# Rounded three-pass matmuls for seven tiles of a state-space input projection, with the places of its input and of its tables' scratch exchanged

## The chip, the cores and the metric

The kernel runs on one core of one Trainium2 chip. A core has a matrix engine (TensorE, PE in the profile; its weight loads are listed as PEld), VectorE (DVE), ScalarE (ACT), GpSimd (POOL) and SyncE (SP), which here only issues transfers. Each engine works through its own queue of instructions in order and waits for others by semaphores. The on-chip memory is SBUF; matmuls write into PSUM, and the other engines read their results from there. The metric is the device time of one execution in microseconds; the median of several runs counts.

## The reference, cut to what matters

Two residual layers, the first with a state-space mixer, the second with attention, each followed by a gated convolutional network. The model width is 1024 and the sequence 512 long, all in float32. The part that the change touches is the very first sub-layer:

```python
def modulate(x, g, shift, scale):
    return rmsnorm(x, g) * (1.0 + scale) + shift

def s5_mixer(h, w_in, lam_re, lam_im, log_dt, b_re, b_im, c_re, c_im, d_skip, w_glu, w_out):
    u = h @ w_in
    ug = u.reshape(Bsz, S, S5_GROUPS, S5_GROUP)
    dt = jnp.exp(log_dt.astype(f32))[:, None]
    mag = jnp.exp(lre * dt)
    lb_re = mag * jnp.cos(lim * dt)
    lb_im = mag * jnp.sin(lim * dt)
    ...
    _, ys = lax.scan(chunk_step, h0, u_chunks)
    y = y + d_skip.astype(f32) * u.astype(f32)
    y = jax.nn.gelu(y)
    y = y * jax.nn.sigmoid(y @ w_glu.astype(f32))
    return (y @ w_out.astype(f32)).astype(h.dtype)
```

Here `h` is `modulate(x, ...)`, its shift and scale are products of the conditioning vector with a large matrix `ada_w`, and 64 groups of 16 channels drive 64 complex states each. `u = h @ w_in` (512 x 1024 by 1024 x 1024) is the input projection.

## The kernel before

Activations lie with channels on the 128 partitions and the 512 positions along the row: eight tiles (KT) of 128 channels. Most products of the kernel are made in three rounded passes. `put_parts` (line 234) rounds a float32 weight tile to a high part on ScalarE (line 236, tile `w_hi`) and takes the rest on VectorE (line 237, `w_lo`). The activations are split in the same way into `a_hi` and `a_lo`. Then `mms` (line 253) adds high by high, high weight by low activation and low weight by high activation in PSUM, three matmuls of type float32r where one float32 matmul would be written. In the profile a float32 matmul shows as two records and a float32r one as one.

The state-space mixer is `s5`. It starts with a head whose order on TensorE, ScalarE, VectorE and SyncE is the order of the program text (`tc.manual_schedule`). Everything behind that is put in order by a scheduler at build time, with program order as the priority; within the `behind` blocks its instructions stay behind the last ones of the head on their engine.

The head, in order:

- x (tile `h`, in the slot `a_lo`) is loaded, its squares are summed over channels on TensorE (line 912).
- `s5_params` (a generator) makes the state parameters on VectorE in three parts: first exponentials, cosine and sine in rings of scratch tiles, then k and the first powers of the complex factor by `cmul` (lines 676 to 681), up to its yield; then the last powers, `lr`, `li` and `mag8`.
- `ada_pe` makes a third of the modulation from `ada_w` on TensorE (line 176), with two loads of 512 KB a step; its last step copies rows out on ScalarE (line 183), and `ada_columns` turns them (lines 132 and 137) into the columns `ga` (line 142, VectorE) and `par` (line 145, ScalarE).
- VectorE makes x without the shift, `a_x` (line 928), eight instructions of 128x512.
- Tile 0 of the projection is done from this x in float32 (line 942), between the steps of the second `ada_pe`, which makes the shift. Once `par` is there, a product of the weights with the shift (line 953, one column) makes up for the missing shift of tile 0, and ScalarE adds the shift to x in place (lines 950 and 961).
- `s5_tables` makes the first three levels of the rotation tables on VectorE (lines 728 to 730).

Tiles 1 to 7 of the projection are made by `inputs(m)` from the shifted x in float32, eight matmuls each (line 972). The result goes to DRAM and comes back turned (`u`). The step of tile m consists of `s5_inputs` (three products on VectorE, lines 762 and 766, tile `x`, then small matmuls on TensorE, line 778, which ScalarE copies out, lines 785 and 789, and VectorE finishes, line 790), `s5_scan` (line 817 on TensorE, lines 828 to 849 on VectorE, a scan at 839), `s5_states_out` (lines 742 and 751, VectorE) and `s5_outputs` of the tile before (lines 859 and 867 on TensorE, a gelu at 873). In even steps VectorE also makes three more levels of tables for the next eight pairs. The modulation of the next sub-layers (line 176 again) is spread over the steps. At the end `parts` splits the outputs into `a_hi` and `a_lo` (lines 989 and 990), `glu_head` starts the next product on them (line 1001, three passes) and makes its low weights (line 998, from the high ones of line 1028).

Room: `raw`, `w_hi` and `w_lo` are rings of 3, 5 and 5 buffers, shared by weights, their parts and the loads of `ada_w`. `raw(..., n)` picks the ring. The weights of tile m of the projection are loaded into ring m % 3 and read there by TensorE. `a_hi` and `a_lo` are one slot each.

Of the kernel before, what the change touches and what calls it, by code (L numbers as in the profile page):

```python
# [8 lines left out]
F32 = mybir.dt.float32  # L9
F32R = mybir.dt.float32r  # L10
I32 = mybir.dt.int32
AF = mybir.ActivationFunctionType
# [5 lines left out]
P = 128  # L18
# [4 lines left out]
G = 64  # L23
# [566 lines left out]
class S5(Trunk):  # L590
# [3 lines left out]
    def s5_consts(self, pool, tp):  # L594
        nc = self.nc
        H = G // 2

        self.bb = pool.tile([P, H, 3, CG], F32, name="s5_bb")
        b = tp.tile([P, H, 2, CG], F32, name="s5_b")
        nc.sync.dma_start(b, self.io["s5_b"])  # L600
        self.s5_b = b
# [23 lines left out]
    def s5_params(self, pool, tp, prm, stats):  # L625
# [8 lines left out]
        keep = lambda n: tp.tile([P, H], F32, name=f"s5_{n}")  # L634
        ring = lambda n: tp.tile([P, (24, 36, 24)[n], H], F32, name=f"s5_ring{n}")
        e = Ew(nc, tp, P, H, "e", ring=ring(0))
# [46 lines left out]
        for n in (1, 2, 4):  # L683
            if n == 4:
                yield
            a, b = slice(8 - n, 8), slice(8 - 2 * n, 8 - n)
            cmul(pr[:, b], pi[:, b], pr[:, a], pi[:, a], pr[:, 8 - n], pi[:, 8 - n], [P, n, H])
# [194 lines left out]
    def s5(self, i, nxt):  # L882
# [5 lines left out]
        with ExitStack() as stack:  # L888
# [3 lines left out]
            with ExitStack() as start:  # L892
# [3 lines left out]
                def load_w(m):  # L896
                    w[m] = self.raw([P, KT, P], self.io["s5_w_in"][m], m % 3)

# [3 lines left out]
                zero = tp.tile([L - 1, CG * GM], F32, name="s5_zero")  # L902
                nc.gpsimd.memset(zero, 0.0)
                with tc.manual_schedule(engines={ENG.PE, ENG.Activation, ENG.DVE, ENG.SP}):
                    self.load_x(self.act)
# [28 lines left out]
                    for k in range(KT):  # L934
# [13 lines left out]
                    )  # L948
                    for k in range(2):
                        nc.scalar.activation(x[:, k], x[:, k], AF.Identity, bias=self.par[i][:, k:k + 1])  # L950
                    col = self.aux.tile([P, 1], F32, name="aux")
                    for k in range(KT):
                        last_mm = nc.tensor.matmul(
                            col, w[0][:, k, :], self.par[i][:, k:k + 1], start=(k == 0), stop=(k == KT - 1)
                        )
                    shifted = self.small.tile([P, 1], F32, name="u_shift")
                    nc.scalar.activation(shifted, col, AF.Copy)
                    first = self.tmp.tile([P, L, B], F32, name="uf", tag="nm_t")
                    nc.scalar.activation(first, ps.rearrange("p (b j) -> p j b", j=L), AF.Identity, bias=shifted)
                    for k in range(2, KT):  # L960
                        nc.scalar.activation(x[:, k], x[:, k], AF.Identity, bias=self.par[i][:, k:k + 1])
                    behind = [self.s5_signs_c(), next(params), self.s5_tables(slice(0, G // 2), 0, 3), last_mm.ins]
            pool = self.s5r = spool("s5r", stack)
            us, ws, w2s, sts = {}, {}, {}, {}

            def inputs(m):
                if m:
                    if m > 1:
                        load_w(m)
                    ps = self.mm.tile([P, S], F32, name="mmp")  # L970
                    for k in range(KT):
                        nc.tensor.matmul(ps, w[m][:, k, :], x[:, k], start=(k == 0), stop=(k == KT - 1))  # L972
                    uf = self.tmp.tile([P, L, B], F32, name="uf", tag="nm_t")
# [414 lines left out]
```

## Time and profile before

| | us |
|---|---|
| median of 3 runs | 1279.46 (1279.35 to 1281.21) |
| the profiled execution | 1280.95 |
| its span, first to last instruction | 1279.2 |
| PE busy | 1256.0 |
| DVE busy | 773.4 |
| ACT busy | 509.9 |

The profile lists one execution. "Busy" is time in which an engine had an instruction in work; matmuls overlap and their ends are modelled, so a busy PE isn't always one at its peak. The chain of waits is followed back from the last instruction, at each step to what released it or to the instruction before it on its engine. Groups list the instructions of one line, engine and shape, with busy time and mean duration, and the idle time in front of them with what ended it. Windows list the busy time of each engine in a stretch, and the TensorE clock that was granted there (1.00 is full speed).

### The profile page before, as it was taken

What the parts mean: (1) busy time and instruction counts of PE and PEld (TensorE: products, weight loads), DVE (VectorE), ACT (ScalarE), POOL (GpSimd) and SP (SyncE); (2) the same over time, 40 slices, a digit from 0 to 9 for tenths busy, and PEclk for the clock granted to TensorE, in tenths of its full rate; (3) what the DMA queues carried; (4) which work ended last, traced back from release to release, by engine and by line L of the source; (5) the groups of instructions that cost most, each with busy time, mean ns of one, the idle gap of its engine ahead of it and who ended that gap; (6) DMA issues with size and microseconds to landing.
All of it is one profiled execution on the core that took longest, in us unless ns stands there. A gap on an engine that the chain in (4) does not pass through costs nothing.

```text
span 1279.2 us, 17722 instructions
## 1 busy us (share of the span) xinstructions
PE 1256.0 (98%) x6822; PEld 1010.0 (79%) x6822; DVE 773.4 (60%) x1398; ACT 509.9 (40%) x929; POOL 56.6 (4%) x103
## 2 busy tenths in 40 slices
PE   7999999999999999999999999999999999999997
PEld 2566678897877878788899887878988888888887
DVE  8988877478664546764566576655754433444443
ACT  2544455334333223332333566553543322333331
POOL 0000000000000000000000343330000000000000
PEclk9999899999999999999999999999999999999999
DMA  9677666337654645643404433323132233332221
GB/s 370 226 228 248 205 212 219 99 107 246 209 177 130 219 137 193 214 146 116 152 3 132 157 125 123 105 70 99 55 129 93 68 91 128 99 99 82 68 80 67
DMA packets 73060, 183.13 MB, mean 143 GB/s; under 512 B 23079, under 2 KB 25471, under 8 KB 71951
## 3 DMA queue, kind: packets, MB, share of 16 engines
q1 hardware_dynamic: 72687, 181.46, 43.9%
q8 instruction: 54, 0.88, 0.3%
q10 hardware_dynamic: 288, 0.52, 0.1%
q14 instruction: 31, 0.25, 0.1%
HBM read 175.04 MB, written 6.92 MB: 142 GB/s over the span
## 4 chain that ended last, share of the span: by engine, by line
PE 94%; DVE 3%; ACT 2%; DMA 1%; issue 1%; SPq 0%; DVEq 0%; ACTq 0%
PE mmp L253 71%; PE mmp L972 4%; PE mmp L1134 3%; PE aux L778 2%; PE mmp L1001 2%; PE aux L1276 2%; PE mmp L176 1%; PE aux L1259 1%; PE aux L867 1%; PE aux L859 1%; PE aux L1229 1%; DVE w_lo L237 1%; PE mmp L912 1%; PE aux L817 1%; PE mmp L942 1%
## 5 line engine op out<-in xcount | busy, mean ns | idle before, releaser
L253 PE MATMUL mmp<-a_hi,w_hi 128*128 128x512 f32 (+1 forms) x912 | 347.1, 382 | 1.0 <-ACT nm_t L1059 0.7
L253 PE MATMUL mmp<-a_hi,w_lo 128*128 128x512 f32 (+1 forms) x912 | 345.1, 379 | 0.0
L253 PE MATMUL mmp<-a_lo,w_hi 128*128 128x512 f32 (+1 forms) x912 | 344.9, 379 | 0.0
L236 ACT ACTIVATE w_hi<-raw 128x1024 fp32r<-128x1024 f32 (+3 forms) x197 | 190.1, 968 | 386.9 <-PE mmp L253 351.0
L237 DVE TENSOR_TENSOR w_lo<-raw,w_hi 128x1024 fp32r<-128x1024 f32 (+3 forms) x197 | 218.9, 1113 | 198.9 <-ACT w_hi L236 193.4
L253 PEld LDWEIGHTS mmp<-a_hi,w_hi 128*128 128x128 f32 x912 | 170.9, 188 | 35.8 <-issue 2.5
L253 PEld LDWEIGHTS mmp<-a_hi,w_lo 128*128 128x128 f32 x912 | 171.5, 188 | 32.2
L253 PEld LDWEIGHTS mmp<-a_lo,w_hi 128*128 128x128 f32 x912 | 171.7, 188 | 30.6
L253 PE MATMUL mmp<-ghi,w_hi 128*128 128x512 f32 (+1 forms) x396 | 147.7, 373 | 0.0
L253 PE MATMUL mmp<-glo,w_hi 128*128 128x512 f32 (+1 forms) x396 | 147.1, 371 | 0.0
L253 PE MATMUL mmp<-ghi,w_lo 128*128 128x512 f32 (+1 forms) x396 | 147.0, 371 | 0.0
L319 DVE SCALAR_TENSOR_TENSOR h<-mmp,par,h 128x512 f32<-128x512 f32 (+1 forms) x56 | 37.6, 673 | 97.2 <-PE mmp L253 96.9
L253 PEld LDWEIGHTS mmp<-glo,w_hi 128*128 128x128 f32 x396 | 74.9, 189 | 14.0
L253 PEld LDWEIGHTS mmp<-ghi,w_hi 128*128 128x128 f32 x396 | 74.8, 189 | 14.1
L253 PEld LDWEIGHTS mmp<-ghi,w_lo 128*128 128x128 f32 x396 | 74.8, 189 | 14.1
L204 DVE SCALAR_TENSOR_TENSOR ada_acc<-ada_raw,sc,ada_acc 128x1024 f32<-128x1024 f32 x49 | 62.8, 1281 | 27.7 <-DMA ada_raw<-in_ada_w 27.3
L450 DVE TENSOR_TENSOR conv<-conv,mmp 128x512 f32<-128x512 f32 x44 | 30.0, 686 | 64.2 <-PE mmp L253 61.1
L446 ACT ACTIVATE conv<-conv 128x512 f32<-128x512 f32 x44 | 27.6, 632 | 101.4 <-DVE conv L443 101.4
L443 DVE SCALAR_TENSOR_TENSOR conv<-mmp,conv_wb,conv 128x511 f32<-128x511 f32 (+1 forms) x88 | 65.0, 744 | 2.5 <-ACT conv L441 1.5
L972 PE MATMUL mmp<-a_x,raw 128*128 128x512 f32 x112 | 57.5, 652 | 0.0
L253 PE MATMUL mmp<-v,w_hi 128*128 128x512 f32 (+1 forms) x160 | 43.1, 359 | 2.1 <-ACT v L236 2.1
L1245 ACT ACTIVATE s<-s,mn 128x128 f32<-128x128 f32 (+3 forms) x64 | 35.1, 550 | 10.9 <-DVE mn L1241 10.9
(248 smaller groups left out, 1629.2 us busy)
## 6 DMA issues: line engine op xcount, KB each, us to landing
raw<-in_w_up SPq DMA_DIRECT2D x88, 512.0 KB, 3.5
ada_raw<-in_ada_w SPq DMA_DIRECT2D x56, 512.0 KB, 4.3
raw<-in_ada_w SPq DMA_DIRECT2D x40, 512.0 KB, 6.1
raw<-in_w_down SPq DMA_DIRECT2D x32, 384.0 KB, 3.1
raw<-in_w_down SPq DMA_DIRECT2D x32, 320.0 KB, 2.9
nf<-nfd SPq DMA_DIRECT2D x8, 1152.0 KB, 5.7
raw<-in_fox_qk SPq DMA_DIRECT2D x16, 512.0 KB, 3.7
h<-in_x SPq DMA_DIRECT2D x8, 512.0 KB, 5.6
```

Source lines behind the costliest of these rows:

```text
L204: nc.vector.scalar_tensor_tensor(acc, w, self.sc[:, k:k + 1], acc, op0=ALU.mult, op1=ALU.add)
L236: nc.scalar.activation(hi, src, AF.Copy)
L237: nc.vector.tensor_tensor(lo, src, hi.bitcast(F32), ALU.subtract)
L253: self.last_mm = self.nc.tensor.matmul(o, wt, xt[:, cols], start=(k == 0 and n == 0), stop=(k == nk - 1 and n == 2),)
L319: self.nc.vector.scalar_tensor_tensor(self.h[:, m, cols], ps, self.par[i][:, 16 + m:17 + m], self.h[:, m, cols], op0=ALU.mult, op1=ALU.add,)
L443: nc.vector.scalar_tensor_tensor(t[:, d:], ps[:, :S - d], cw[:, 2 - d, f:f + 1], t[:, d:], op0=ALU.mult, op1=ALU.add)
L446: nc.scalar.activation(t, t, AF.Silu)
L450: nc.vector.tensor_tensor(t, t, ps, ALU.mult)
L778: nc.tensor.matmul(ps[g2][:, j, cols], x[rows, a + j, r].rearrange("p c j -> p (c j)"), self.rr[rows, planes, q, :], start=(j == 0 and r = ...
L972: nc.tensor.matmul(ps, w[m][:, k, :], x[:, k], start=(k == 0), stop=(k == KT - 1))
L1134: self.last_mm = nc.tensor.matmul(ps[q, b][:, :n], xt[:, k, tb], wt, start=(k == 0 and i == 0), stop=(k == KT - 1 and i == 2),)
L1245: nc.scalar.activation(s[:, r], s[:, r], AF.Exp, scale=-1.0, bias=mn[:, r:r + 1], accum_out=sm[:, 0, r:r + 1])
```

## The change

1. `inputs(m)` for tiles 1 to 7 uses three rounded passes. `load_w` always loads into the ring `raw`. `round_w` rounds the weights on ScalarE into `w_hi`, `rest_w` takes the rest on VectorE into `w_lo`. For tiles 2 to 7 the passes run k by k, three for each; tile 1 is done in the head, first both passes with the high weights for each k, then the eight with the low ones.
2. x keeps its float32 form in a tile of its own (`s_x`, in the pool of the head), without the shift. The shifted x is written as `xhi` by ScalarE and `xlo` by VectorE (shift added and high part subtracted in one instruction) into the slots `a_hi` and `a_lo`. The eight activations that added the shift in place are gone; the eight that write `xhi` take their place.
3. The slot `a_hi`, in which x was, first holds `room`, out of which `s5_b` and the scratch rings of `s5_params` are cut. They had tiles of their own.
4. Order in the head: the yield of `s5_params` comes one power earlier (at n == 2), the last step of the shift's `ada_pe` behind the load of tile 1's weights, `s5_c` and the zeros, and behind `round_w(1)`. The third part of `s5_params` and the first level of the tables come ahead of tile 1's projection, the other two levels behind it, and the activations of tile 0's result behind it too.

```diff
-        b = tp.tile([P, H, 2, CG], F32, name="s5_b")
+        (b,) = self.scratch(H * 2 * CG)
+        b = b.rearrange("p (h r c) -> p h r c", r=2, c=CG)
...
-        ring = lambda n: tp.tile([P, (24, 36, 24)[n], H], F32, name=f"s5_ring{n}")
+        rings = [t.rearrange("p (n h) -> p n h", h=H) for t in self.scratch(24 * H, 36 * H, 24 * H)]
+        ring = lambda n: rings[n]
...
         for n in (1, 2, 4):
-            if n == 4:
+            if n == 2:
                 yield
...
                 def load_w(m):
-                    w[m] = self.raw([P, KT, P], self.io["s5_w_in"][m], m % 3)
+                    w[m] = self.raw([P, KT, P], self.io["s5_w_in"][m])
+
+                def round_w(m):
+                    t = self.wpool.tile([P, KT, P], F32R, name="w_hi", bufs=WB)
+                    nc.scalar.activation(t, w[m], AF.Copy)
+                    w[m] = t, w[m]
+
+                def rest_w(m):
+                    t = self.wpool.tile([P, KT, P], F32R, name="w_lo", bufs=WB)
+                    hi, src = w[m]
+                    nc.vector.tensor_tensor(t, src, hi.bitcast(F32), ALU.subtract)
+                    w[m] = hi, t
...
+                room = self.act.tile([P, KT * S], F32, name="s5_room", tag="a_hi")
+                used = [0]
+
+                def scratch(*sizes):
+                    out = []
+                    for n in sizes:
+                        out.append(room[:, used[0]:used[0] + n])
+                        used[0] += n
+                    return out
...
-                    x = self.act.tile([P, KT, S], F32, name="a_x", tag="a_hi")
+                    x = tp.tile([P, KT, S], F32, name="s_x")
...
-                    next(shift)
                     load_w(1)
...
-                    for k in range(2):
-                        nc.scalar.activation(x[:, k], x[:, k], AF.Identity, bias=self.par[i][:, k:k + 1])
+                    round_w(1)
+                    next(shift)
                     col = self.aux.tile([P, 1], F32, name="aux")
...
+                    params = next(params)
+                    self.s5_tables(slice(0, G // 2), 0, 1)
+                    xhi, xlo = (self.act.tile([P, KT, S], F32R, name=n, tag=n) for n in ("a_hi", "a_lo"))
+                    ps1 = self.mm.tile([P, S], F32, name="mmp")
+                    for k in range(KT):
+                        sh = self.par[i][:, k:k + 1]
+                        nc.scalar.activation(xhi[:, k], x[:, k], AF.Identity, bias=sh)
+                        nc.vector.scalar_tensor_tensor(
+                            xlo[:, k], x[:, k], sh, xhi[:, k].bitcast(F32), op0=ALU.add, op1=ALU.subtract
+                        )
+                        for t in (xhi, xlo):
+                            nc.tensor.matmul(ps1, w[1][0][:, k], t[:, k], start=(k == 0 and t is xhi), stop=False)
+                    rest_w(1)
+                    for k in range(KT):
+                        last_mm = nc.tensor.matmul(ps1, w[1][1][:, k], xhi[:, k], start=False, stop=(k == KT - 1))
...
-                    for k in range(2, KT):
-                        nc.scalar.activation(x[:, k], x[:, k], AF.Identity, bias=self.par[i][:, k:k + 1])
-                    behind = [self.s5_signs_c(), next(params), self.s5_tables(slice(0, G // 2), 0, 3), last_mm.ins]
+                    behind = [self.s5_signs_c(), params, self.s5_tables(slice(0, G // 2), 1, 3), last_mm.ins]
...
                     if m > 1:
                         load_w(m)
-                    ps = self.mm.tile([P, S], F32, name="mmp")
-                    for k in range(KT):
-                        nc.tensor.matmul(ps, w[m][:, k, :], x[:, k], start=(k == 0), stop=(k == KT - 1))
+                        round_w(m)
+                        rest_w(m)
+                        ps = self.mm.tile([P, S], F32, name="mmp")
+                        for k in range(KT):
+                            for n, (wt, xt) in enumerate(((0, xhi), (0, xlo), (1, xhi))):
+                                nc.tensor.matmul(
+                                    ps, w[m][wt][:, k], xt[:, k], start=(k == 0 and n == 0), stop=(k == KT - 1 and n == 2)
+                                )
+                    else:
+                        ps = ps1
```

More of the change, by code (lines that the diff above doesn't have):

```diff
@@ L903, in s5 @@
                 nc.gpsimd.memset(zero, 0.0)
+                room = self.act.tile([P, KT * S], F32, name="s5_room", tag="a_hi")
[6 more added lines that the diff above has]
+                    return out
+                self.scratch = scratch
                 with tc.manual_schedule(engines={ENG.PE, ENG.Activation, ENG.DVE, ENG.SP}):
@@ L969, in inputs @@
                         load_w(m)
-                    ps = self.mm.tile([P, S], F32, name="mmp")
-                    for k in range(KT):
-                        nc.tensor.matmul(ps, w[m][:, k, :], x[:, k], start=(k == 0), stop=(k == KT - 1))
+                        round_w(m)
[3 more added lines that the diff above has]
+                            for n, (wt, xt) in enumerate(((0, xhi), (0, xlo), (1, xhi))):
+                                nc.tensor.matmul(
+                                    ps, w[m][wt][:, k], xt[:, k], start=(k == 0 and n == 0), stop=(k == KT - 1 and n == 2)
+                                )
+                    else:
+                        ps = ps1
                     uf = self.tmp.tile([P, L, B], F32, name="uf", tag="nm_t")
```

1 line of the change is left out of this document (removed).

## The prediction

> **What bounds the kernel now.** I read the totals of the page first, then the chain of work that ended last, then the stretch in which the changed lines run.
>
> ```profile
> PE 1256.0 (98%) x6822; PEld 1010.0 (79%) x6822; DVE 773.4 (60%) x1398; ACT 509.9 (40%) x929; POOL 56.6 (4%) x103
> ...
> PE 94%; DVE 3%; ACT 2%; DMA 1%; issue 1%; SPq 0%; DVEq 0%; ACTq 0%
> ```
>
> TensorE (PE) carries 94% of the chain, but that is an average over the whole kernel. The change lies in the state-space stage, so the next view is the chain of waits there (start, length, what; two records of L972 are one full float32 matmul), and beside it the busy time of each engine in two stretches.
>
> ```profile
> 27.92 0.99 PE mmp L176 x8
> ...
> 37.93 1.95 PE aux L953 x16
> 39.88 8.67 PE mmp L972 x16
> 48.55 1.95 PE aux L778 x32
> 50.49 3.63 PE mmp L972 x8
> 54.12 1.95 PE aux L778 x32
> ...
> 125.40 4.49 PE mmp L972 x10
> ...
> 137.12 5.42 PE mmp L972 x6
> ...
> 180.75 1.93 PE aux L867 x32
> 182.68 14.52 PE mmp L1001 x63
> ```
>
> ```profile
> core 0: us, PE busy (x) PEld busy (x) DVE busy (x) ACT busy (x) POOL busy (x), PEclk, DMA share, GB/s
> 25.14:179.11 153.97, 152.75 (x1172) 94.90 (x1173) 132.71 (x219) 73.31 (x212) 0.00 (x0) 0.97 0.71 227
> 90.00:120.00 30.00, 30.00 (x262) 19.21 (x261) 28.48 (x46) 10.51 (x38) 0.00 (x0) 1.00 0.75 230
> ```
>
> From 25.14 us (the modulation of x begins) to 179.11 (the last state scan ends) PE is busy 152.75 of 153.97 us, so PE sets the pace. But VectorE (DVE) is busy 132.71 of it, and from 90 to 120 us 28.48 of 30, 95%. The second engine is close behind the first. The change takes work from PE and gives work to DVE, so what matters is the 21.26 us for which DVE is idle here. Two waits hold half of that:
>
> ```profile
> 125.43 1.23 DVE L762 TENSOR_TENSOR x<-s_lr,s_bb 128x1024 f32<-128x1024 f32 x1 [4.86 <-PE aux L778]
> 144.31 0.29 DVE L790 TENSOR_TENSOR kt<-kt,dd 128x128 f32<-128x128 f32 x1 [4.95 <-ACT kt L789]
> ```
>
> In brackets stands the idle time before the instruction and who ended it: in the timeline DVE waits for products that PE has not made yet (L789 only empties what L778 made). Such waits are the room in which added DVE work can go.
>
> **The change, part by part.** The prices come from these groups (busy, mean ns of one):
>
> ```profile
> L972 PE MATMUL mmp<-a_x,raw 128*128 128x512 f32 x112 | 57.5, 652 | 0.0
> L928 DVE SCALAR_TENSOR_TENSOR a_x<-h,ga,aux 128x512 f32<-128x512 f32 x8 | 5.4, 743 | 0.0
> L730 DVE TENSOR_TENSOR s_rot<-s_tab 128x128 f32<-128x128 f32 (+3 forms) x15 | 6.5, 435 | 0.2
> L998 DVE TENSOR_TENSOR w_lo<-raw,w_hi 128x1024 fp32r<-128x1024 f32 x4 | 4.7, 1266 | 0.0
> L1028 ACT ACTIVATE w_hi<-raw 128x1024 fp32r<-128x1024 f32 x4 | 4.1, 1048 | 0.0
> L961 ACT ACTIVATE a_x<-a_x,par 128x512 f32<-128x512 f32 x6 | 3.8, 710 | 0.0
> ```
>
> *Matmuls.* A float32 tile of eight matmuls takes two pieces like that at 50.49: 2 x 3.63 = 7.26 us. The rounded passes already exist in L1001: 63 in 14.52 us, 0.230 us each. Twenty-four of them make 5.53 us, so a tile saves 1.73 us and tiles 2 to 7 save 10.4. Tile 1 takes 8.67 us now, at a lowered clock for part of it; 24 passes would save 3.1 more. All told PE loses 13.5 us of work. Smaller pieces between other matmuls could cost up to 0.2 us a piece, as the float32 ones do now (3.63 for four and 4.49 for five, so 0.86 each and 0.19 for the piece), or nothing; I take nothing, since PE will not be the bound.
>
> *Rounding on DVE.* rest_w is an L998: 4.7 / 4 = 1.17 us, seven times 8.2 us. The low half of x is a scalar_tensor_tensor of the shape of L928: 5.4 us for eight. Nothing leaves DVE. It gains 13.6 us.
>
> *Rounding on ACT.* round_w is an L1028, 1.05 us, seven times 7.3 us. The eight activations that add the shift stay (they write xhi and not x in place). ACT is busy 73.31 of 153.97 us, so the 7.3 us lie in its idle time; without that cover they would delay the emptying of L778's tiles by 1.05 us a step, which is one reason why I allow DVE idle time below.
>
> *The start of the stage.* These timeline rows carry the steps of the head:
>
> ```profile
> 22.82 1.03 PE L137 MATMUL aux<-sel,ada_rows 128*128 128x2 f32 x8
> 23.50 0.27 DVE L676 TENSOR_TENSOR s_w<-s_pr 128x64 f32<-128x64 f32 x1
> 24.94 0.16 DVE L142 SCALAR_TENSOR_TENSOR ga<-aux,rest 128x8 f32<-128x8 f32 x1
> 25.14 5.36 DVE L928 SCALAR_TENSOR_TENSOR a_x<-h,ga,aux 128x512 f32<-128x512 f32 x8
> 26.19 0.44 SPq L157 DMA_DIRECT2D raw<-in_s_w_in  x1
> 30.41 0.38 DVE L676 TENSOR_TENSOR s_w<-s_pr 128x128 f32<-128x128 f32 x1
> 35.91 1.05 ACT L606 ACTIVATE s_bb<-s_b 128x1024 f32<-128x1024 f32 x1
> 37.70 0.18 ACT L145 ACTIVATE par<-aux 128x8 f32<-128x8 f32 x1 [0.75 <-PE aux L137]
> 36.83 0.25 DVE L728 TENSOR_TENSOR s_tab<-s_rot,s_turn 128x64 f32<-128x64 f32 x1
> 42.05 1.22 DVE L766 TENSOR_TENSOR x<-x,x 128x1024 f32<-128x1024 f32 x1
> ```
>
> The yield at n == 2 takes the six instructions of 23.50 to 24.94 from ahead of ga (L142). PE's L137 ends at 23.85, so ga can run at about 24.0 and L928 start at 24.2, 0.9 us earlier. The six are not gone: 1.44 us later in the same queue. A new wait stands in ACT: round_w(1) ahead of the copy of par (L145). Behind it wait par's copy, the column product L953 and the eight xhi. With the earlier start L606 ends near 36.0, round_w(1) near 37.1 and par near 37.3, against 37.88 now. So this costs nothing as long as the weight has landed. Its load now needs one of the three raw buffers, of which one comes free when the L176 at 27.92 is done, so it is issued near 28 instead of 26.19, with s5_c, the zeros and tile 2's weights queued behind it on SP.
>
> ```profile
> raw<-in_s_w_in SPq DMA_DIRECT2D x4, 512.0 KB, 7.2
> ```
>
> At 7.2 us it lands near 35.5. A landing 2 us later would push par by 1.5 us; a quicker one gains nothing. I take zero. The loads of tiles 2 to 7 are as many as before, only in another ring. Scratch in x's old room makes xhi wait until the last table parameter is made; that is L928 from 24.2 to 29.5, the moved 1.4 us and the 6.4 us from 30.41 to 36.83, so about 37.3, next to par.
>
> From there DVE has eight xlo (5.4 us; xhi on ACT, 0.71 us each by L961, keeps step), rest_w(1) 1.2, the three tables, which now take 2.8 us (36.83 to the first product of tile 0 at about 39.6), and three products of tile 0 like L766, 3.7: 37.3 + 5.4 + 1.2 + 2.8 + 3.7 = 50.4. Now L766 is ready at 43.3. So DVE is 7 us late at this point, and L778 of tile 0 starts at 50.4 and not at 48.55: PE loses 1.8 us there, although tile 1's projection ends earlier. What is late next is tile 1's tables on DVE and its L778 (54.12).
>
> **The sum** is a count of DVE. Busy 132.7 + 13.6 + 1.4 moved in = 147.7 us, from 24.2: without any idle time the last scan ends at 171.9, with PE's own 179.1 - 13.5 = 165.6 below that. So DVE becomes the bound, and the question is its idle share. Bounds: none (171.9, 7.2 us gained) and the 13.8% of now. From 90 to 120 us it was 5%, but there PE was full as well. With PE relieved I take 3%: 147.7 / 0.97 = 152.3, end at 176.5, 2.6 us earlier. At 4.6% nothing is gained (147.7 of the 154.9 us from 24.2 to 179.1); at 8% the stage ends 5.6 us later.
>
> Behind the last scan the stage ends like this:
>
> ```profile
> 178.38 0.73 DVE L849 TENSOR_TENSOR ua<-ua,ub 128x512 f32<-128x512 f32 x1
> 182.76 0.66 ACT L873 ACTIVATE yg<-aux 128x256 f32<-128x256 f32 x2 [5.52 <-issue]
> 190.70 1.18 ACT L989 ACTIVATE a_hi<-yt 128x512 fp32r<-128x512 f32 x1 [5.94 <-DMA yt<-s_yd]
> 191.91 1.17 DVE L990 TENSOR_TENSOR a_lo<-yt,a_hi 128x512 fp32r<-128x512 f32 x1 [5.94 <-ACT a_hi L989]
> ```
>
> L867 of tile 7 starts 1.64 us after that scan, since PE is full. With a freer PE between 0 and 1.64 us of it go; I take 0.4. What follows (gelu, two trips through memory, L989, L990) hangs on it and moves along; L1001 (14.52 us) covers it. From there to the end PE is the bound and untouched. Total: 3.0 us earlier. The profiled execution took 1280.95 us (span 1279.2 and 1.75 around it), so 1277.95 by it; the median of the runs is 1279.46, 1.49 lower, which gives **1276.5**.
>
> **Rivals.** (A) DVE runs almost without waiting, since it is the late engine and everything it needs is ready: 5 to 8.5 us gained, 1272.5. For it: from 90 to 120 us DVE waits for only 1.5 of 30 us even with PE full. Against: in each step DVE needs PE's L817 and L778 in turn. (B) The head's lateness is never made up: L778 of tile 1 needs DVE's next tables and three more products (3.7) after 50.4. The tables are three instructions a level: L730 and its two partners take 3 x 6.5 = 19.5 us, less the 2.8 of the head, in four sets, 4.2 us each. That makes 58.3 against 54.12, 4.2 us late, and the chain L766 to L778 to the next L762 hands that on to every step: 1283.5. It decides as soon as DVE's idle share stays above 4.6%; for it speak the 5% of that stretch. (C) The clock:
>
> ```profile
> 136.00:137.00 1.00, 1.00 (x6) 0.91 (x5) 1.00 (x3) 1.00 (x5) 0.00 (x0) 0.50 0.97 359
> ```
>
> PE was granted half its clock here, and the three float32 matmuls at 137.12 took 5.42 us where 0.19 + 3 x 0.86 = 2.77 is usual. A PE that waits for DVE in the head and in the steps may be slowed like this oftener; two or three such pieces of 2.65 us, while DVE waits for them, turn 3.0 us of gain into 2 to 5 of loss: 1282.5. The Trainium skill, page "TensorE: Matmul & The Clock Gate", section "Why this matters for your kernels", warns of PE idle gaps over about 3 us, after which the clock halves. The row agrees only with the halving: PE counted as busy all through that microsecond, so the trace does not show that idling is the trigger.
>
> **How the numbers follow.** Forecast (idle 2 to 4%, 1.5 to 5 us gained) 0.45; A 0.15; B 0.28; C 0.12. A measurement of this kernel tells 0.2% (2.6 us) from no change. Of the forecast's share 0.30 lies beyond it and 0.15 within. With A, faster is 0.45; with 0.03 of B and 0.02 of C, same is 0.20; the rest, 0.35, is slower. The forecast's own range is 1274 to 1279. The range for 8 in 10 reaches from A's far side (8.5 us gained, 1271) to 8% idle (5.6 us lost, 1285).
>
> **What would show it.** In the changed profile: 24 passes of a tile near 0.23 us each; rest_w near 1.2 us; L928 starting near 24.2; tile 0's L778 near 50.4; DVE over 95% busy from 24 to the last scan, with the waits of 4.86 and 4.95 us gone; the last L849 ending near 176.5. I am wrong if DVE keeps gaps of microseconds in the first four steps, if PE's half clock shows up at more than two places, or if anything behind 200 us moves by itself.

## The result, and the profile after

| | before | after |
|---|---|---|
| median of 5 runs, us | 1279.35 (1278.35 to 1281.21) | 1289.65 (1288.75 to 1290.14) |
| ratio, 95% interval | | 1.0078 (1.0064 to 1.0092) |
| profiled execution, us | 1280.95 | 1288.75 |
| its span, us | 1279.2 | 1287.0 |
| mean granted clock of TensorE over the span | 0.993 | 0.985 |

The change made the kernel 10.3 us slower; 1276.5 was forecast, in a range of 1271 to 1285. Line numbers of the changed kernel are higher: L778 is L780 there, L817 is L819, L859 is L861, L867 is L869, L849 is L851, L762 and L766 are L764 and L768, L972 is L1011, L1001 is L1044, and the weights are rounded in L903 and L909.

The groups of the changed kernel first (busy us, mean ns of one), then its windows:

```profile
L1011 PE MATMUL mmp<-a_hi,w_hi 128*128 128x512 f32 x48 | 20.1, 419 | 0.0
...
L909 DVE TENSOR_TENSOR w_lo<-raw,w_hi 128x1024 fp32r<-128x1024 f32 x7 | 8.5, 1217 | 0.0
...
L903 ACT ACTIVATE w_hi<-raw 128x1024 fp32r<-128x1024 f32 x7 | 7.4, 1054 | 2.3 <-DMA raw<-in_s_w_in 2.3
...
L986 DVE SCALAR_TENSOR_TENSOR a_lo<-s_x,par,a_hi 128x512 fp32r<-128x512 f32 x8 | 5.4, 748 | 0.7 <-ACT a_hi L985 0.7
```

```profile
core 0: us, PE busy (x) PEld busy (x) DVE busy (x) ACT busy (x) POOL busy (x), PEclk, DMA share, GB/s
24.24:190.00 165.76, 156.98 (x1251) 114.14 (x1244) 146.16 (x240) 79.49 (x219) 0.00 (x0) 0.90 0.67 214
...
72.00:82.00 10.00, 9.27 (x56) 8.25 (x56) 8.44 (x16) 5.06 (x15) 0.00 (x0) 0.50 0.45 140
150.00:160.00 10.00, 6.03 (x64) 4.38 (x61) 10.00 (x20) 3.39 (x11) 0.00 (x0) 0.87 0.86 257
160.00:170.00 10.00, 10.00 (x88) 7.96 (x88) 8.22 (x12) 5.30 (x19) 0.00 (x0) 0.50 0.74 236
170.00:180.00 10.00, 10.00 (x64) 7.52 (x64) 6.21 (x12) 4.92 (x9) 0.00 (x0) 0.61 0.41 133
```

The added instructions cost what was forecast. The clock column is new: 0.90 over the stage against 0.97 before, and half over tens of us. Added up from windows of 1 us between 24 and 214 us, 34 us ran at half clock (41 to 45, 72 to 82, 157 to 178) against 10 before (40 to 44, 136 to 143).

Two places set the loss. The first is the step of tile 1. L817 (L819) of tiles 0 and 1 in the timeline, before and after, with DVE's wait for it after, and the chain of waits after between them:

```profile
61.48 1.15 PE L817 MATMUL aux<-u,w 128*64 128x64 f32 x32
...
79.85 0.80 PE L817 MATMUL aux<-u,w 128*64 128x64 f32 x18
```

```profile
62.41 1.15 PE L819 MATMUL aux<-u,w 128*64 128x64 f32 x32
...
69.92 1.12 PE L780 MATMUL aux<-s_rr,x 64*128 64x80 f32 x16 [1.81 <-DVE x L768]
...
72.84 3.68 PE L869 MATMUL aux<-ua,w 64*128 64x63 f32 x32 [0.73 <-DVE ua L851]
...
87.42 0.80 PE L819 MATMUL aux<-u,w 128*64 128x64 f32 x18
...
89.85 0.69 DVE L830 TENSOR_TENSOR m<-aux,s_rot 128x512 f32<-128x512 f32 x1 [4.72 <-PE aux L819]
```

```profile
71.05 1.14 DVE w_lo L909
72.18 0.61 DVE ua L851
72.84 3.68 PE aux L869 x32
76.52 1.73 PE aux L780 x14
78.25 7.08 PE mmp L1011 x22
85.33 1.84 PE mmp L176 x12
87.49 0.72 PE aux L819 x18
```

The step is 25.0 us and was 18.4. PE waits for DVE at 68 and 72, while 22 of the 24 passes of a tile stand further back in its queue; they then run as one block (7.08 us, the first part at half clock) ahead of L819, for which DVE waits 4.72 us. The changed kernel then stays late: at L819 of tiles 2, 3 and 4 by 5.8, 5.6 and 4.9 us (103.60 against 97.82, 119.46 against 113.91, 135.66 against 130.81). At tile 5 it is ahead, with L861 at 150.43 and its counterpart at 152.01, because the kernel before needs 20.1 us for that step, with half clock from 136 to 143, and the changed one 13.7. The second place follows there. PE's rows, before and after, and the last scan's end on DVE after:

```profile
152.01 2.00 PE L859 MATMUL aux<-u,t 128*128 128x64 f32 x16
...
173.08 2.00 PE L867 MATMUL aux<-ua,w 64*128 64x63 f32 x32
```

```profile
150.43 2.00 PE L861 MATMUL aux<-u,t 128*128 128x64 f32 x16
152.35 1.92 PE L176 MATMUL mmp<-raw,sc 128*32 128x512 f32 x14
158.24 3.67 PE L869 MATMUL aux<-ua,w 64*128 64x63 f32 x32 [3.97 <-DVE ua L851]
...
163.69 3.71 PE L780 MATMUL aux<-s_rr,x 64*128 64x80 f32 x32
...
169.23 3.68 PE L861 MATMUL aux<-u,t 128*128 128x64 f32 x16
...
181.94 2.00 PE L869 MATMUL aux<-ua,w 64*128 64x63 f32 x32
...
189.30 0.69 DVE L851 TENSOR_TENSOR ua<-ua,ub 128x512 f32<-128x512 f32 x1
```

PE runs out of work, waits 3.97 us, and finds its clock halved. Every small group then takes twice its time (3.67 where 2.00 is usual), and from tile 5's L861 to tile 6's L869 it takes 31.5 us, which took 21.1. That is 10.4 us, and nothing behind it wins them back: the last L851 ends at 189.99 (179.11), and L253, the first matmul behind the stage, starts at 208.81 (199.60).

### The profile page after: what moved, and what is told of

Same layout as the page of the kernel before. It is cut to its first block, busy times and chain, and to the rows that moved or that the text cites. A ratio compares the mean times of both kernels' runs of the same rounds, so it can differ in the third digit from the quotient of the medians.

```text
span 1287.0 us, 17839 instructions
## 1 busy us (share of the span) xinstructions
PE 1255.6 (98%) x6878; PEld 1025.4 (80%) x6878; DVE 784.7 (61%) x1413; ACT 515.9 (40%) x936; POOL 56.2 (4%) x103
## 4 chain that ended last, share of the span: by engine, by line
PE 84%; DVE 7%; ACT 4%; DMA 3%; issue 1%; POOL 0%; SPq 0%; DVEq 0%; POOLq 0%
PE mmp L253 68%; PE mmp L1177 3%; PE mmp L1011 2%; ACT s L1288 2%; PE aux L1319 2%; PE aux L869 1%; PE aux L780 1%; PE aux L1302 1%; PE aux L861 1%; DVE w_lo L237 1%; PE mmp L1044 1%; PE mmp L936 1%; PE mmp L176 1%; DMA nf<-nfd 1%; PE aux L819 1%
## 5 line engine op out<-in xcount | busy, mean ns | idle before, releaser
L253 PE MATMUL mmp<-a_hi,w_hi 128*128 128x512 f32 (+1 forms) x912 | 347.1, 382 | 2.1 <-ACT nm_t L1102 1.8
L253 PE MATMUL mmp<-a_hi,w_lo 128*128 128x512 f32 (+1 forms) x912 | 345.0, 379 | 0.0
L253 PE MATMUL mmp<-a_lo,w_hi 128*128 128x512 f32 (+1 forms) x912 | 344.9, 379 | 0.0
L253 PEld LDWEIGHTS mmp<-a_hi,w_hi 128*128 128x128 f32 x912 | 170.8, 188 | 37.1 <-issue 2.6
L253 PEld LDWEIGHTS mmp<-a_hi,w_lo 128*128 128x128 f32 x912 | 171.5, 188 | 32.1
L253 PEld LDWEIGHTS mmp<-a_lo,w_hi 128*128 128x128 f32 x912 | 171.7, 188 | 30.7
L253 PE MATMUL mmp<-ghi,w_hi 128*128 128x512 f32 (+1 forms) x396 | 147.7, 373 | 0.0
L253 PE MATMUL mmp<-glo,w_hi 128*128 128x512 f32 (+1 forms) x396 | 147.1, 371 | 0.0
L253 PE MATMUL mmp<-ghi,w_lo 128*128 128x512 f32 (+1 forms) x396 | 147.0, 371 | 0.0
L253 PEld LDWEIGHTS mmp<-ghi,w_hi 128*128 128x128 f32 x396 | 74.8, 189 | 14.1
L253 PEld LDWEIGHTS mmp<-glo,w_hi 128*128 128x128 f32 x396 | 74.9, 189 | 14.0
L253 PEld LDWEIGHTS mmp<-ghi,w_lo 128*128 128x128 f32 x396 | 74.8, 189 | 14.1
L253 PE MATMUL mmp<-v,w_hi 128*128 128x512 f32 (+1 forms) x160 | 42.1, 352 | 2.1 <-ACT v L236 2.1
L311 ACT ACTIVATE nm_t<-h 128x512 f32<-128x512 f32 (+1 forms) x36 | 19.0, 532 | 48.5 <-DVE h L319 48.2
```

What stands on the lines that cost most here:

```text
L253: self.last_mm = self.nc.tensor.matmul(o, wt, xt[:, cols], start=(k == 0 and n == 0), stop=(k == nk - 1 and n == 2),)
```

## The experiments

Each edit is planned anew at build time: the scheduler puts all instructions behind the head into another order, so a run tests the edit together with its new order. "Half clock" is counted in the one profiled execution, as above; "step" is from L819 of tile 0 to that of tile 1; "end" is the start of L253 behind the stage. Each ratio is taken against executions of the kernel before that belong to the same batch; their medians lie between 1279.27 and 1280.02.

| run | median us (runs) | ratio, 95% interval | half clock us | step us | end us |
|---|---|---|---|---|---|
| before | 1279.35 (5) | 1 | 10 | 18.4 | 199.6 |
| after | 1289.65 (5) | 1.0078 (1.0064 to 1.0092) | 34 | 25.0 | 208.8 |
| e1 dense matmuls in the gap | 1282.81 (10) | 1.0026 (1.0012 to 1.0039) | 24 | 25.1 | 205.4 |
| e2 head only | 1277.6 (10) | 0.9982 (0.9971 to 0.9992) | 7 | 16.4 | 196.1 |
| e3 two passes | 1275.08 (7) | 0.9959 (0.9945 to 0.9973) | 44 | 16.2 | 197.2 |
| e4 low part on GpSimd | 1287.08 (4) | 1.0062 (1.0046 to 1.0077) | 34 | 18.4 | 207.2 |
| e5 dense in both gaps | 1287.52 (5) | 1.0064 (1.0051 to 1.0076) | 14 | 20.7 | 206.3 |
| e6 no rest | 1274.25 (5) | 0.9954 (0.9942 to 0.9967) | 17 | 18.4 | 192.6 |
| e7 DVE work alone | 1277.33 (11) | 0.9985 (0.9975 to 0.9994) | 3 | 16.7 | 197.4 |
| e8 head, exact | 1277.35 (11) | 0.9986 (0.9974 to 0.9998) | 10 | 16.4 | 196.1 |
| e9 rest unread | 1280.55 (11) | 1.0002 (0.9983 to 1.0022) | 34 | 17.3 | 203.7 |
| e10 low passes last | 1291.89 (5) | 1.0098 (1.0077 to 1.0119) | 41 | 21.1 | 209.9 |
| e11 early, low last | 1281.5 (11) | 1.0014 (0.9998 to 1.0029) | 34 | 18.3 | 200.9 |
| e12 as e11, dense | 1284.76 (6) | 1.0039 (1.0026 to 1.0052) | 14 | 18.2 | 204.3 |
| e13 early alone | 1285.35 (11) | 1.0032 (1.0014 to 1.0049) | 24 | 20.8 | 200.9 |

### The clock

**e1** puts unused matmuls into PE's gap behind L861 of tile 5.

```diff
+WARM = {5: 5}
...
+        if WARM.get(m):
+            full = self.mm.tile([P, S], F32, name="mmp")
+            with self.tc.issue_after(mm.ins):
+                for _ in range(WARM[m]):
+                    nc.tensor.matmul(full, self.ones, self.rr[:, 1].rearrange("p q c -> p (q c)"), start=True, stop=True)
```

> The changed kernel with five more float32 matmuls of 128x512 (results not used) on TensorE behind L861 of tile 5, in the 4 us in which TensorE has nothing to do (154.3 to 158.2 us). Clock theory: the loss is the half clock from 157.7 to 177.4 that follows this gap, 18.4 us of work there that takes 10 at full clock; with the gap filled the clock stays at 1.00 and 7 to 9 us come back: 1281 to 1283. VectorE theory: the stage is late because VectorE has 13.6 us more to do, and TensorE would wait for it at any clock; then the time stays within 2 us of 1289.6.

PE's timeline at the second place, and its windows (L862 and L875 are L861 and L869 there):

```profile
154.58 2.00 PE L862 MATMUL aux<-u,t 128*128 128x64 f32 x16
156.41 4.51 PE L870 MATMUL mmp<-s_rr,ones 128*128 128x512 f32 x10
...
162.70 2.00 PE L875 MATMUL aux<-ua,w 64*128 64x63 f32 x32
...
168.99 2.00 PE L862 MATMUL aux<-u,t 128*128 128x64 f32 x16
...
179.14 2.00 PE L875 MATMUL aux<-ua,w 64*128 64x63 f32 x32
```

```profile
150.00:160.00 10.00, 10.00 (x113) 7.28 (x106) 10.00 (x19) 5.27 (x20) 0.00 (x0) 1.00 0.66 197
160.00:170.00 10.00, 9.77 (x124) 6.42 (x123) 10.00 (x15) 7.72 (x24) 0.00 (x0) 1.00 0.79 265
170.00:180.00 10.00, 9.74 (x86) 6.95 (x85) 10.00 (x17) 7.01 (x14) 0.00 (x0) 1.00 0.80 262
```

With five unused matmuls (4.5 us) in the gap, the clock stays at 1.00, and the stretch from L862 to the next tile's L875 takes 24.6 us where it took 31.5, the added matmuls included. So this one halving cost about 7 us in the stretch itself, not the 2 to 3 pieces of 2.65 of rival C. The median falls by 6.8 us, which agrees, but e1's order differs elsewhere too: its profiled execution (1286.82 us, mean clock 0.988) halves at 91 and 111, where the changed kernel doesn't, and its last scan ends only 1.9 us sooner (188.06). The seven executions with a mean clock of 0.992 to 0.994 took 1280.56 to 1283.56 us, the three at 0.987 to 0.989 took 1285.08 to 1287.33.

**e5** adds two more of them behind L861 of tile 0.

```diff
-WARM = {5: 5}
+WARM = {0: 2, 5: 5}
```

> As e1_dense_in_gap, with two more unused float32 128x512 matmuls behind L861 of tile 0, ahead of the half clock that the changed kernel shows from 72 to 82 us. Clock theory (each drop costs its own time, and a drop is set off by a PE that has run out of work): no half clock from 70 to 82, and 1 to 3 us less than the 1282.8 of e1, 1280 to 1282. DVE theory (DVE sets the pace there, so a slow PE up to 82 us costs nothing and the two matmuls add up to 2 us): 1282.8 to 1285.

The diff is against e1. The half clock of 72 to 82 is gone and 13.6 us are left in all, yet the time is 4.7 us above that of e1, beyond what either theory allowed. In its new order the third step is 20.8 us long (L820 at 98.6 and 119.4), PE idles 1.9 of the ten us from 100, and half clock comes at 104 instead. The unused matmuls move the trouble. That says nothing on the price of the drop at 72.

### Head, passes and GpSimd

**e2** leaves the head as changed and gives tiles 2 to 7 back to float32 (from the high part of x; its low part is left out for these tiles).

```diff
-                        round_w(m)
-                        rest_w(m)
...
+                            nc.tensor.matmul(ps, w[m][:, k], xhi[:, k].bitcast(F32), start=(k == 0), stop=(k == KT - 1))
```

> The head of the changed kernel with tile 1 in three passes, but tiles 2 to 7 in float32 from the raw weights and the rounded high part of x; the low parts are left out for these tiles. VectorE has 6.6 us more than before and not 13.6. VectorE theory: about half the loss, 1284 to 1286. Clock theory: the long float32 matmuls keep TensorE from idling in the later steps, so only the head's own delay is left, 1279 to 1283, and no half clock after 150 us. If the head by itself is the cause: 1287 or more.

The head alone gains, and 1277.6 lies below all three cases. **e8** is the same with all of x: float32 x stays in its place, shifted behind the first tile, and the low part for tile 1 lies in `w_lo` buffers.

```diff
-                    x = tp.tile([P, KT, S], F32, name="s_x")
+                    x = self.act.tile([P, KT, S], F32, name="a_x", tag="a_hi")
...
+                    for k in range(KT):
+                        nc.scalar.activation(x[:, k], x[:, k], AF.Identity, bias=self.par[i][:, k:k + 1])
...
+                            nc.tensor.matmul(ps, w[m][:, k], x[:, k], start=(k == 0), stop=(k == KT - 1))
```

> As e2_head_only, tiles 2 to 7 in float32 and tile 1 in three rounded passes, but with the whole float32 x for tiles 2 to 7: x stays in its old room, shifted in place on ACT behind the first tile, the rounded part of x goes into the other room, its low part into four buffers of the rounded weights, and the tables' scratch is back in its own place. If e2's gain is that of the head: 1276.5 to 1279. If it came from what e2 leaves out (eight activations on ACT less): 1279 to 1281.

It computes all that the kernel before computes and takes 0.9986 of its time (0.9974 to 0.9998). Its window over the stage, in which PE stays full:

```profile
25.00:190.00 165.00, 162.91 (x1266) 107.11 (x1267) 146.68 (x239) 82.21 (x225) 0.00 (x0) 0.97 0.74 241
```

The head with tile 1 in three passes is worth some 2 us; the loss lies in tiles 2 to 7.

**e3** leaves out the third pass of these tiles and their rest_w (the low part of the weights).

```diff
-                        rest_w(m)
...
-                            for n, (wt, xt) in enumerate(((0, xhi), (0, xlo), (1, xhi))):
+                            for n, (wt, xt) in enumerate(((0, xhi), (0, xlo))):
```

> Tiles 2 to 7 without the third pass: neither the low part of the weights (six VectorE instructions of 1.2 us) nor its matmuls (48 of 0.23 us) are made. VectorE theory: VectorE is relieved of 7.2 us, so 6 to 8 us come back, 1282 to 1284. Clock theory: TensorE has even less to do and still waits; where the scans are ready earlier than the fillers run out, the clock stays and it is 1275 to 1280, otherwise the half clock stays and it is 1288 to 1290. The granted clock after 150 us tells which.

It is the second fastest of all, with 44 us of half clock, for which the clock theory had named 1288 to 1290. So half clock alone doesn't decide the order of different kernels: here PE has 48 passes less (11 us at 0.23) and DVE 7.2 us less, and a slow PE may have time to spare.

**e4** moves rest_w to GpSimd.

```diff
-                    nc.vector.tensor_tensor(t, src, hi.bitcast(F32), ALU.subtract)
+                    nc.gpsimd.tensor_tensor(t, src, hi.bitcast(F32), ALU.subtract)
```

> The low part of the weights of tiles 1 to 7 made by GpSimd instead of VectorE: seven instructions of 1.2 us leave VectorE. VectorE theory: 1281 to 1283, if GpSimd needs under 4 us each. Clock theory: the same only where TensorE's waits go away with it; if a wait of about 4 us stays, the half clock stays and so does most of the loss. A GpSimd that slows VectorE beside it would show in longer VectorE instructions.

A group and some rows of e4. In the changed kernel L764 and L768 take 1.2 us each:

```profile
L909 POOL TENSOR_TENSOR w_lo<-raw,w_hi 128x1024 fp32r<-128x1024 f32 x7 | 17.4, 2499 | 103.6 <-ACT w_hi L903 68.2 <-ACT par L145 35.4
...
47.89 2.39 POOL L909 TENSOR_TENSOR w_lo<-raw,w_hi 128x1024 fp32r<-128x1024 f32 x1 [8.14 <-ACT w_hi L903]
47.94 3.42 DVE L764 TENSOR_TENSOR x<-s_lr,s_bb 128x1024 f32<-128x1024 f32 x1
...
106.37 2.67 POOL L909 TENSOR_TENSOR w_lo<-raw,w_hi 128x1024 fp32r<-128x1024 f32 x1 [15.96 <-ACT w_hi L903]
107.32 0.68 DVE L831 TENSOR_TENSOR m<-aux,s_rot 128x512 f32<-128x512 f32 x1
107.92 2.21 DVE L768 TENSOR_TENSOR x<-x,x 128x1024 f32<-128x1024 f32 x1
```

GpSimd takes twice DVE's time, and DVE is not relieved: an instruction of DVE that starts while GpSimd subtracts, with both of its inputs in SBUF, ends only behind it. Seven do so here and take 11.2 us longer together, more than the 8.5 us of rest_w that left; L830 and L831, which read one input (`aux`) from PSUM, keep their 0.68 us. So e4 doesn't test what less work on DVE would bring: from 24 to 188 us DVE is busy 149.2 us, more than the 146.2 of the changed kernel's stage. PE still idles (6.39 of ten us busy from 150) and half clock stays at 34 us. Its median is 2.6 us lower, with overlapping intervals of the ratios.

### DVE's work, and the wait for it

**e7** is the kernel before with as much added on DVE, read by nobody.

```diff
+                    if m > 1:
+                        t = self.act.tile([P, KT, P], F32R, name="spare", tag="a_lo")
+                        nc.vector.tensor_tensor(t, w[m], w[m], ALU.subtract)
```

> The kernel before, with one unused tensor_tensor of 128x1024 on DVE for each of the tiles 2 to 7, where the change has rest_w: 7.2 us more on DVE and all of PE's float32 work kept. DVE theory: DVE is 95% busy from 90 to 120 us already, so most of the 7.2 us reach the end of the stage: 1283 to 1286, half clock no more than the 10 us of before. Cover theory (DVE's idle 21 us take them as long as PE is dense): 1279.5 to 1281. Clock theory: as cover theory as long as no new half clock appears, and 3 to 5 us more for each new drop.

Groups and windows of e7:

```profile
L900 DVE TENSOR_TENSOR spare<-raw 128x1024 fp32r<-128x1024 f32 x6 | 7.3, 1220 | 0.0
```

```profile
130.00:140.00 10.00, 10.00 (x94) 6.87 (x87) 6.75 (x12) 5.12 (x19) 0.00 (x0) 1.00 0.92 273
140.00:150.00 10.00, 10.00 (x96) 6.07 (x94) 9.67 (x17) 4.82 (x13) 0.00 (x0) 1.00 0.78 230
```

7.3 us more on DVE cost nothing while PE has its float32 work: PE stays at 10.00 of ten, and the order that came of it even lacks the halving at 136 to 143. It came out faster than every case expected of it, so the amount of DVE work is not by itself the cause.

**e6** takes rest_w of tiles 2 to 7 out of the changed kernel and leaves PE its 24 passes, the third with the rounded weights again (the product of the low weights is left out).

```diff
-                        rest_w(m)
...
-                            for n, (wt, xt) in enumerate(((0, xhi), (0, xlo), (1, xhi))):
+                            for n, (wt, xt) in enumerate(((0, xhi), (0, xlo), (0, xhi))):
```

> The changed kernel without rest_w of tiles 2 to 7; the third pass multiplies the rounded weights once more, so PE has as many passes as in the changed kernel and DVE 7.2 us less. The low part of these weights is left out. DVE theory (the extra DVE work is what costs): 7 us less than the changed kernel, 1281 to 1283, with whatever half clock there is. Clock theory (the drop of 157 us comes from a PE that runs out of work while DVE is late): with DVE earlier the gap of 3.97 us before L869 of tile 5 closes and the drop with it: 1276 to 1279. If the drop comes from PE having too little work whatever DVE does: the half clock stays, and 1284 or more.

It is the fastest of all, 0.46% below the kernel before and below all three cases: passes in place of float32 are no loss where DVE doesn't make their low part, and no half clock is left between 88 and 193 us.

**e9** keeps rest_w and has only the second of these edits.

> The changed kernel with rest_w of tiles 2 to 7 still made on DVE, but read by nobody: the third pass multiplies the rounded weights once more, as in e6_no_rest. The product of the low weights is left out. It tells the amount of DVE's work from the wait for it. Amount theory (7.2 us more on DVE cost what e6 gains, whoever waits): 1286 to 1290, as the changed kernel. Wait theory (what costs is that the passes of a tile stop at their third matmul until DVE comes to rest_w, so PE lacks them as filling between the products and does them in one block later, ahead of L819 of tile 1): 1273 to 1278, step of tile 1 (L819 of tile 0 to L819 of tile 1) 18 to 19 us and not 25.

From the changed kernel to e9 the ratio falls by 0.76% (9.7 us), from e9 to e6 by another 0.48% (6.1 us). So about 6 us hang on the amount of work and 10 on its being read, in the orders that were built for it. L819 in e9:

```profile
63.26 1.97 PE L819 MATMUL aux<-u,w 128*64 128x64 f32 x32
...
80.57 1.15 PE L819 MATMUL aux<-u,w 128*64 128x64 f32 x32
```

17.3 us and not 25: with nobody waiting for `w_lo`, the passes fill PE between the products, and no block stands ahead of L819. But e9's 34 us of half clock are as many as those of the changed kernel, and its median missed the 1273 to 1278 of the wait theory. The wait is a part of the cause, not all of it.

**e10** puts the passes that need `w_lo` last, **e11** also takes the weights one tile ahead, **e13** has the lead alone.

```diff
+                            for n, xt in enumerate((xhi, xlo)):
+                                nc.tensor.matmul(ps, w[m][0][:, k], xt[:, k], start=(k == 0 and n == 0), stop=False)
+                        for k in range(KT):
+                            nc.tensor.matmul(ps, w[m][1][:, k], xhi[:, k], start=False, stop=(k == KT - 1))
```

```diff
+                        for n in ((2, 3) if m == 2 else (m + 1,)):
+                            if n < KT:
+                                load_w(n)
+                                round_w(n)
+                                rest_w(n)
```

> The changed kernel with the same 24 passes of a tile in another order: first high and low x by the high weights for all eight k, then the eight with w_lo, as tile 1 has it already. Nothing is left out. Wait theory: 16 of 24 passes need no rest_w and serve as filling, and no block of passes stands ahead of L819 of tile 1: 1276 to 1281. Amount theory: DVE has as much to do as before, 1286 to 1290. Clock theory: better by what half clock is gone, 1280 to 1286.

> As e10_low_last, and weights are loaded, rounded and their rest taken one tile ahead of their passes. Nothing is left out. Wait theory: what e10 leaves of the wait goes too, 1274 to 1279; it could give back where the load ahead holds a raw buffer that the modulation's loads need. Amount theory: 1286 to 1290.

> The changed kernel with the weights loaded, rounded and their rest taken one tile ahead, the passes in their order (high, low, w_lo for each k). Nothing is left out. Wait theory: the lead is what removes the wait for rest_w, so the step of tile 1 is 18 to 20 us and the time that of e11_early_low_last, 1280 to 1283. If only both together help: 1286 or more.

The order alone (e10) doesn't help: a step of 21.1 us, 41 us of half clock, a median above all three cases, and an interval that overlaps the changed kernel's. Both together (e11) win 0.64% back, to a value between the two theories. For e13 neither case came out clearly: its step is 20.8 us, its median lies between the cases, and its 11 runs lie between 1276.80 and 1288.17. The timeline and windows of e11:

```profile
142.67 1.98 PE L819 MATMUL aux<-u,w 128*64 128x64 f32 x32
144.57 3.68 PE L861 MATMUL aux<-u,t 128*128 128x64 f32 x16
...
175.56 2.00 PE L869 MATMUL aux<-ua,w 64*128 64x63 f32 x32
```

```profile
130.00:140.00 10.00, 8.48 (x100) 5.99 (x96) 10.00 (x17) 4.01 (x17) 0.00 (x0) 0.99 0.95 303
140.00:150.00 10.00, 10.00 (x82) 8.03 (x80) 8.73 (x18) 4.48 (x12) 0.00 (x0) 0.50 0.52 170
150.00:160.00 10.00, 8.33 (x61) 6.80 (x58) 9.46 (x13) 6.38 (x17) 0.00 (x0) 0.50 0.58 185
```

L861 of tile 5 is 7.4 us ahead of the kernel before (144.57 against 152.01), part of which is the half clock of the latter from 136 to 143. Under half clock, from 140 to 171, the lead goes: L869 of tile 6 is 2.5 us behind (175.56 against 173.08). That the halving alone takes it isn't shown.

**e12** puts unused matmuls before and into that stretch.

```diff
+WARM = {3: 3, 4: 4, 5: 4}
...
+        if WARM.get(m):
...
+                for _ in range(WARM[m]):
```

> As e11_early_low_last, with 3, 4 and 4 unused float32 128x512 matmuls behind the last L861 of tiles 3, 4 and 5, ahead of and inside the stretch of 31 us of half clock (140 to 171 us) of e11. Clock theory: e11 was 8 us ahead of the kernel before at L819 of tile 5 (142.7 against 150.9) and lost it at half clock; without it 5 to 8 us of this stay, less some of the 9.5 us of added matmuls: 1273 to 1278. DVE theory (DVE's work sets the end of the stage, half clock or not): 1281 to 1284.

The half clock of 140 to 171 is gone, but the new order lets PE wait 4.75 us for a product of DVE at 102 (PE busy 4.33 of the ten us from 100), and half clock comes from 104 to 117. Its 1284.76 lies above both cases. With 9.5 us of unused matmuls besides, this can't test the price, and no run here keeps e11's lead.

### The same instructions at another clock

Every run lists its mean granted clock, and runs of one kernel have the same instructions in the same order. e13, us and clock of its runs:

```
1276.80 0.994   1280.06 0.992   1280.82 0.988   1282.33 0.989   1284.87 0.986   1285.35 0.987
1285.93 0.987   1286.11 0.987   1286.50 0.983   1287.69 0.982   1288.17 0.983
```

A straight line through them rises by 0.90 us for each 0.001 of clock that is lacking (correlation 0.93). For the other kernels with ten or more runs it is 0.47 (e7) to 0.89 (e1), and for the kernel before 0.91 to 1.17 in its four batches. The mean clock of the changed kernel's profiled run is 0.008 below that of before. By these slopes that is 4 to 9 of the 10.3 us, a rough estimate, since its own 5 runs lie too close (0.983 to 0.986) to show a slope and the two kernels are different programs. Runs alone can't say which way it goes either, for a PE that waits longer may be slowed by that; e1 speaks for the clock as the cause, for there it was held over one stretch and this stretch became shorter.

## Why the prediction was wrong

- **Durations and amounts: right.** L952, the modulation of x, starts at 24.24 (24.2 forecast); the passes of 78.25 to 85.33 run at 0.23 us each once the clock is back; rest_w is 1.22 us; DVE is busy 146.2 us in the stage (147.7). DVE's lateness in the head was right too: L780 of tile 0 at 51.09 (50.4), of tile 1 at 59.39, near rival B's 58.3.
- **The failed step: "I take 3%" for DVE's idle share.** That is 4.6 us. From 24.24 to 190.0 DVE idles 19.6 us of 165.8, 11.8%, close to the 13.8% of before, where PE set the pace. The 15.0 us more, less the 1.5 that DVE works less than forecast, are the 13.5 by which the last scan (189.99) misses the forecast 176.5. The 3% assumed that a PE with less work has its results ready whenever DVE asks. Instead PE works through an order fixed at build time, and where it runs out of work its clock halves. DVE's waits at the two places (1.56 and 4.72 us, then 1.06, 0.72 and 3.79) are 11.9 of its 19.6 us. Two of the signs of being wrong came true: DVE has gaps of 4.72 and 2.10 us in the early steps, and half clock shows at three places. The same idle share rules out rival A.
- **Rival B** named the right start, and its lateness lasted to tile 4 (4.9 us at L819). But the head is not what makes it: e2 and e8, which have the same head, are faster than before. The step of tile 1 does, with the passes that stand behind rest_w.
- **Rival C** had a part of the mechanism, with too small a price. It priced half clock by pieces of 2.65 us, two or three of them. It lasted 20.5 us at one place, over groups that all double, and e1 shows about 7 us for that place alone. In the last steps before 175 us PE never idled in the kernel before, which had float32 matmuls to fill with; filled with passes it runs out at 154. The Trainium skill, page "TensorE: Matmul & The Clock Gate", section "Why this matters for your kernels", puts the limit at idle gaps of about 3 us. The 3.97 us gap here agrees; in e11 the halving came at 140 behind gaps of 1.09 and 0.41 us among small matmuls, which that limit doesn't cover, and in the kernel before it came at 136.0 with PE busy for 98% of the 3.4 us ahead of it.
- **Neither half of the change in tiles 2 to 7 costs by itself.** Passes without rest_w gain (e6, 0.9954, with a product left out), as much work on DVE beside float32 costs nothing (e7, 0.9985), and both together lose (1.0078). With less to fill PE, DVE's added work decides when PE goes on. That is what the pairs show; each has an order of its own. round_w on ACT and the loads into one ring stay in e6, so these are not what costs.
- **Not foreseen: rest_w as a term that PE waits for.** The prediction counted its 1.2 us on DVE and not its place: it stands in DVE's queue among the products, the passes that read it stand in PE's, and what is behind them waits. e9 prices reading it at 9.7 us, and its work beside passes at 6.1; both include what follows by the clock and the new orders, so these don't add up with the 7 us of e1. How the 10.3 us split between order and clock stays open: each edit changes both.
- **Behind the stage** no new cost appears: the last scan ends 10.9 us later, L253 starts 9.2 us later, and the span is 7.8 longer. The last 1.4 us lie within what runs of one kernel differ by (2.9 us in the five of before).

## What to carry to other kernels

Work taken from the engine that sets the pace and work given to the second one have to be priced together: here the first alone gained (e6), the second alone cost nothing (e7), and both lost 0.78%. The float32 matmuls were slow, but they needed nothing of DVE and filled PE while DVE was late. Before replacing one product by three on a second engine's parts, look where the parts are made in that engine's queue and who stands behind the first reader; where the second engine is already 95% busy over stretches, change only the part that gains by itself, as with tile 1 here (0.9986). And compare the granted clock of the runs before comparing their times.

## What the runs showed of the hardware

- The clock changes on a grid. In all fifteen traces every stretch of half clock from 24 to 214 us is 1 to 9 whole steps of 3.41 us (3.42, 10.24 and 20.48 us in the changed kernel, 3.42 and 6.82 in the one before), and the stretches of one trace lie on one grid (those that start at 72.02 and 157.36 are 25 steps apart).
- Half clock is not lifted by a PE that the profile shows as busy. In the changed kernel it lasted from 157.4 to 177.8 us, over L869, L780, L819 and L861, with PE at 10.00 of ten us from 160. It went at the end of the step in which L1044 began (176.60), and at the first place at the end of a step filled with L1011 (78.2 to 82.3), both dense 128x512 passes. Nor does the busy share tell when it comes: the changed kernel kept its clock behind a step at 48.1 with PE busy for 59% of it, the kernel before lost it behind one with 98%.
- Runs of one kernel differ by up to 12 us with the clock they were granted: the kernel before took 1275.66 us at a mean of 0.999 and 1287.70 at 0.989, on one core.
- A tensor_tensor of 128x1024 on GpSimd takes 2.50 us, where DVE takes 1.22. A DVE instruction with both inputs in SBUF that starts beside it waits for its end (L764 3.42 us and not 1.22, one of 128x32 2.31 us and not 0.19); one that reads an input from PSUM doesn't (0.68 us as always).
